# Low parts of feed-forward weights by an accumulating DMA instead of a VectorE subtraction

## The chip, the cores and the metric

The kernel runs on one core of a Trainium2 chip, in one launch. The metric is the device time of a run in microseconds; the median of three runs stands for a kernel.

## What is computed

Two layers of a diffusion block over 256 latent and 256 context tokens, 1024 wide, in float32. Each layer has a feed-forward, a mixer (attention, neighbourhood attention and a short convolution) and a second feed-forward; the context tokens take no part in the last feed-forward. Two conditioning vectors give scales, shifts and gates (`w_ada`). What the change touches is the feed-forward:

```python
def swiglu(u, wi, wo):
    g, up = jnp.split(u @ wi, 2, axis=-1)
    return (jax.nn.silu(g) * up) @ wo
...
h = post(h, swiglu(pre(h, m, 0, 0), ffn_wi[0], ffn_wo[0]), m, 0, 1, 0.5)
hc = post(hc, swiglu(pre(hc, mc, 0, 0), ffn_wi[0], ffn_wo[0]), mc, 0, 1, 0.5)
...
h = post(h, swiglu(pre(h, m, 6, 4), ffn_wi[1], ffn_wo[1]), m, 6, 5, 0.5)
if not last:
    hc = post(hc, swiglu(pre(hc, mc, 6, 4), ffn_wi[1], ffn_wo[1]), mc, 6, 5, 0.5)
```

The hidden width is 2816, that is 22 blocks of 128.

## The kernel before

Matrix products are made in the format float32r, which holds fewer bits than float32. So each float32 operand is split into a rounded half (high) and what rounding left over (low), and a product is three matmuls into one PSUM bank: high by high, low by high, high by low.

**Weights** come in units of 128 x 1024 elements (512 KB). A unit is a slot of a ring of eight (`next_slot`, tile `w`, 128 x 2 x 1024). `load_unit` brings the float32 unit into a staging buffer by a transfer on SyncE's queue (L91), ScalarE casts it to the rounded half `w[:, 0]` (L93), and VectorE subtracts that from the staging buffer into the low half `w[:, 1]` (L94). There are two staging buffers (`stg`), and in the last feed-forward three others (`stgx`). The transfer needs only a free staging buffer; the cast needs a free slot, which TensorE gives back after the last matmul that reads it.

**A feed-forward** (`ffn`) is called four times: over four token tiles (512 columns) for both of the first layer and the first of the second layer, and over two tiles (256 columns) for the last. The hidden blocks f go in groups of four. `up_all` loads the units of a pair of blocks (`load_up`: for each f the gate unit u = 0 and the value unit u = 1) and makes 24 matmuls for each unit. `down` multiplies a finished group of four blocks by its output weights, two units for each half of the output. Steadily the order is: up of two blocks (four units), down of a group (four units), up of two blocks (four units). The first four blocks are made otherwise: in the first two calls by `up_all`, in the last two by `up_first`, which takes eight token-major units (`wi_tm`) that fill the whole ring. Beside this VectorE accumulates the products of the conditioning (`ada_step`, L159 and L161) for the stages to come.

**Other engines.** GpSimd computes the reciprocal roots of the norms (L99, L111) and issues a few transfers (L192, L210). TensorE's transposes go through tiles `ptr`; PSUM banks are `mm` (3), `at` (2) and `pv` (1), taken in turn by the feed-forward. The order of instructions on every engine is chosen by a planner that simulates the kernel (`schedule_with_timeline_sim=True`); each engine then takes its instructions strictly in that order.

Of the kernel before, what the change touches and what calls it, by code (L numbers as in the profile page):

```python
# [8 lines left out]
F32 = mybir.dt.float32  # L9
F32R = mybir.dt.float32r  # L10
BF16 = mybir.dt.bfloat16
AF = mybir.ActivationFunctionType
ALU = mybir.AluOpType
# [12 lines left out]
def tile_hybrid_block(ctx: ExitStack, tc: tile.TileContext, xin, c2, w_ada, w_ada0, bcol, grow, gcol, win, qkg, bias_in,  # L26
                      convw, woa, wi, wi_tm, wo, ident, rope, out):
    nc = tc.nc
    pe, act, dve, pool, sp = nc.tensor, nc.scalar, nc.vector, nc.gpsimd, nc.sync
# [51 lines left out]
    def next_slot():  # L81
        return ring.tile([128, 2, 1024], F32R, name="w", tag="w")
# [3 lines left out]
    def load_unit(src):  # L86
        if more_stg:
            s = more_stg[0].tile([128, 1024], F32, name="stgx", tag="stgx", bufs=3)
        else:
            s = stg.tile([128, 1024], F32, name="stg", tag="stg")  # L90
        sp.dma_start(out=s, in_=src)  # L91
        w = next_slot()
        act.copy(w[:, 0], s)  # L93
        dve.tensor_tensor(out=w[:, 1], in0=s, in1=w[:, 0].bitcast(F32), op=ALU.subtract)  # L94
        return w

    def rsum(ss):
# [197 lines left out]
    def ffn(ph, l, i, U, tiles, after, ada_target, mode):  # L295
# [3 lines left out]
        ada0 = ada_done[0]  # L299

        def load_up(fs):
            return {(f, u): load_unit(wi[l, i, f, u]) for f in fs for u in range(2)}

        def up(fs, ws, segs, c0, n):
            pss = {(f, u): cur["mm"]() for f in fs for u in range(2)}
# [25 lines left out]
        def up_all(fs, mode=""):  # L331
            if mode == "k":
                segs = [(2 * qd, 2, lo_c, n_c) for qd in range(4)]
            elif mode[0:3] == "tok":
                segs = [(0, 8, 256, 256), (0, 8, 0, 256)]
            else:
                segs = [(0, 8, lo_c, n_c)]
            up(fs, load_up(fs), segs, lo_c, n_c)

        def load_down(f0, nf, hf):  # L340
            return [load_unit(wo[l, i, (f0 + fp) // 2, hf]) for fp in range(0, nf, 2)]
# [32 lines left out]
        def up_first():  # L374
            wt = [[load_unit(wi_tm[l, i, u, kp]) for kp in range(4)] for u in range(2)]
            for f in range(4):
                acts[f] = ph.tile([128, 2, n_c], F32R, name="a", tag="a", bufs=6)
            for t in tiles:
                c = slice(128 * t, 128 * t + 128)
                p = [tm_block(U, t, wt[u]) for u in range(2)]  # L380
                sg = ph.tile([128, 512], F32, name="sg", tag="sg")
                act.activation(sg, p[0], AF.Silu)
                dve.tensor_tensor(out=sg, in0=p[1], in1=sg, op=ALU.mult)
                pt = ps_tr.tile([128, 4, 128], F32, name="ptr", tag="ptr")
                for f in range(4):
                    pe.transpose(pt[:, f], sg[:, 128 * f:128 * f + 128], I)  # L386
                for f in range(4):
                    act.copy(acts[f][:, 0, c], pt[:, f])
                    dve.tensor_tensor(out=acts[f][:, 1, c], in0=pt[:, f], in1=acts[f][:, 0, c].bitcast(F32),
                                      op=ALU.subtract)  # L390
# [9 lines left out]
        for g, (f0, nf) in enumerate(FGROUPS[:-1]):  # L400
            f1 = f0 + nf
            if f1 < 20:
                up_all([f1, f1 + 1])
            elif len(tiles) == 4:
                wup = load_up([20, 21])
                up([20, 21], wup, [(0, 8, 256, 256)], 256, 256)
            else:
                up_all([20, 21])
            down(f0, nf, {}, [[(t, hf)] for hf in range(2) for t in tiles], g == 0, False)
            if f1 < 20:  # L410
                up_all([f1 + 2, f1 + 3])
# [379 lines left out]
```

## Time and profile before

| | |
|---|---|
| median of three runs | 1717.47 us (1716.42 to 1718.55) |
| profiled execution | 1717.2 us, span of the core 1715.4 us |
| mean granted TensorE clock | 0.995 |
| TensorE matmul, busy | 1684.8 us, 98% |
| VectorE, busy | 1200.1 us, 70% |
| ScalarE, busy | 715.0 us, 42% |
| GpSimd, busy | 49.0 us, 3% |
| DMA engines, SyncE's queue | 43.7% of 16 engines' span |

The time of the profiled execution is the span from the first to the last instruction and 1.8 us around it. Matmuls are pipelined and their ends are modelled, so TensorE's busy time shows where it had work, not how well it used it. A name such as L94 is a line of the kernel; `w<-stg,w` reads "tile w is written from tiles stg and w".

### The profile page before, as it was taken

How to read it: one execution, taken by the hardware profiler on the slowest of the kernel's cores; microseconds unless marked ns; L12 is line 12 of the kernel's file. 1: busy time of each engine (PE TensorE's matmuls, PEld its weight loads, DVE VectorE, ACT ScalarE, POOL GpSimd, SP SyncE). 2: the span in 40 equal slices, each digit the busy share in tenths (PEclk: the TensorE clock that was granted, in tenths of full speed). 3: DMA queues.
4: the chain of work that ended last, by engine and by line, in shares of the span. 5: the costliest groups of instructions: out<-in, count | busy, mean ns of one | idle time of the engine just before them, and what ended most of it. 6: DMA issues, size and time to landing. Idle time of an engine off the chain costs nothing.

```text
span 1715.4 us, 23300 instructions
## 1 busy us (share of the span) xinstructions
PE 1684.8 (98%) x9098; PEld 1413.9 (82%) x9098; DVE 1200.1 (70%) x1723; ACT 715.0 (42%) x1243; POOL 49.0 (3%) x76
## 2 busy tenths in 40 slices
PE   6999999999999999999999999999999999989997
PEld 4888888888877788888888888888888888769997
DVE  3578788877766675486686657889785768756664
ACT  5432222227656573322222354322222657765442
POOL 1000000002000010000000010000000110000000
PEclk9999999999999999999999999999999999999999
DMA  8566555523121334464443225656463323346551
GB/s 315 175 221 199 182 189 187 170 90 111 62 76 48 93 112 148 146 197 144 163 161 134 75 99 197 203 189 198 161 206 112 113 78 121 114 158 217 178 195 64
DMA packets 75613, 257.31 MB, mean 150 GB/s; under 512 B 10976, under 2 KB 14256, under 8 KB 74992
## 3 DMA queue, kind: packets, MB, share of 16 engines
q1 hardware_dynamic: 74304, 250.29, 43.7%
q0 software_dynamic: 1200, 5.55, 0.9%
q8 instruction: 71, 1.16, 0.3%
q14 instruction: 38, 0.31, 0.1%
HBM read 254.71 MB, written 1.09 MB: 149 GB/s over the span
## 4 chain that ended last, share of the span: by engine, by line
PE 96%; DMA 1%; DVE 1%; ACT 1%; issue 0%; POOL 0%; SPq 0%; DVEq 0%; POOLq 0%; ACTq 0%
PE mm L79 51%; PE at L79 27%; PE pv L79 15%; PE ptr L590 2%; PE ptr L234 1%; DMA GT<-in_qkg_dram 1%; DMA H<-in_xin_dram 0%; DMA stg<-in_wi_tm_dram 0%; DVE H L280 0%; DVE w L94 0%; ACT junk L217 0%; PE ptr L79 0%; PE ptr L471 0%; PE ptr L386 0%; ACT xn L229 0%
## 5 line engine op out<-in xcount | busy, mean ns | idle before, releaser
L79 PE MATMUL mm<-Uh,w 128*128 128x512 f32 (+1 forms) x1808 | 486.9, 348 | 0.0
L93 ACT CAST w<-stg 128x1024 fp32r<-128x1024 f32 x262 | 274.5, 1050 | 463.1 <-PE mm L79 398.4
L94 DVE TENSOR_TENSOR w<-stg,w 128x1024 fp32r<-128x1024 f32 x262 | 319.4, 1220 | 164.7 <-ACT w L93 163.9
L79 PEld LDWEIGHTS mm<-Uh,w 128*128 128x128 f32 x1808 | 318.7, 189 | 43.6 <-issue 1.9
L79 PE MATMUL mm<-Ul,w 128*128 128x512 f32 (+1 forms) x904 | 315.0, 348 | 0.0
L161 DVE SCALAR_TENSOR_TENSOR acc<-adas,S,acc 128x1024 f32<-128x1024 f32 x217 | 269.1, 1278 | 6.6 <-DMA adas<-in_w_ada_dram 6.3
L79 PE MATMUL at<-Uh,w 128*128 128x512 f32 (+1 forms) x960 | 253.7, 344 | 0.7 <-ACT Uh L272 0.7
L79 PE MATMUL mm<-w,a 128*128 128x512 f32 x924 | 228.1, 390 | 0.0
L79 PEld LDWEIGHTS mm<-w,a 128*128 128x128 f32 x924 | 173.1, 188 | 35.7
L79 PEld LDWEIGHTS mm<-Ul,w 128*128 128x128 f32 x904 | 171.2, 189 | 21.5 <-issue 0.5
L79 PEld LDWEIGHTS at<-Uh,w 128*128 128x128 f32 x960 | 168.9, 190 | 22.6 <-ACT Uh L272 0.9
L79 PE MATMUL mm<-w,Uh 128*128 128x512 f32 (+1 forms) x544 | 172.1, 389 | 0.0
L79 PE MATMUL at<-Ul,w 128*128 128x512 f32 (+1 forms) x480 | 165.4, 345 | 1.0 <-DVE Ul L273 1.0
L79 PE MATMUL at<-w,a 128*128 128x512 f32 x594 | 147.6, 391 | 0.0
L79 PEld LDWEIGHTS at<-w,a 128*128 128x128 f32 x594 | 110.8, 188 | 23.2 <-ACT a L325 0.8
L79 PE MATMUL pv<-Uh,w 128*128 128x512 f32 (+1 forms) x464 | 127.7, 353 | 0.0
L79 PEld LDWEIGHTS mm<-w,Uh 128*128 128x128 f32 x544 | 100.7, 188 | 19.8 <-issue 0.7
L94 DVE TENSOR_TENSOR w<-stgx,w 128x1024 fp32r<-128x1024 f32 x58 | 71.0, 1224 | 53.7 <-ACT w L93 53.6
L79 PE MATMUL mm<-w,Ul 128*128 128x512 f32 (+1 forms) x272 | 105.3, 387 | 0.9 <-DVE Ul L253 0.9
L320 DVE TENSOR_TENSOR sg<-mm,sg 128x512 f32<-128x512 f32 (+1 forms) x86 | 51.1, 594 | 75.4 <-PE mm L79 74.0
L79 PEld LDWEIGHTS at<-Ul,w 128*128 128x128 f32 x480 | 90.9, 189 | 12.6 <-DVE Ul L273 1.7
L79 PEld LDWEIGHTS pv<-Uh,w 128*128 128x128 f32 x464 | 82.7, 189 | 11.9
(162 smaller groups left out, 1807.9 us busy)
## 6 DMA issues: line engine op xcount, KB each, us to landing
adas<-in_w_ada_dram SPq DMA_DIRECT2D x144, 512.0 KB, 4.0
stg<-in_wi_dram SPq DMA_DIRECT2D x124, 512.0 KB, 4.2
stg<-in_wo_dram SPq DMA_DIRECT2D x66, 512.0 KB, 3.3
stg<-in_win_dram SPq DMA_DIRECT2D x40, 512.0 KB, 3.2
stgx<-in_wi_dram SPq DMA_DIRECT2D x36, 512.0 KB, 4.2
stgx<-in_wo_dram SPq DMA_DIRECT2D x22, 512.0 KB, 4.2
stg<-in_woa_dram SPq DMA_DIRECT2D x16, 512.0 KB, 3.3
stg<-in_wi_tm_dram SPq DMA_DIRECT2D x16, 512.0 KB, 3.3
```

The lines of the kernel that those rows point to most:

```text
L79: pe.matmul(out, lhsT=lhsT, rhs=rhs, start=first, stop=last)
L93: act.copy(w[:, 0], s)
L94: dve.tensor_tensor(out=w[:, 1], in0=s, in1=w[:, 0].bitcast(F32), op=ALU.subtract)
L161: dve.scalar_tensor_tensor(out=acc[:, v], in0=s, scalar=S[:, kt, v:v + 1], in1=acc[:, v], op0=ALU.mult, op1=ALU.add)
L234: pe.transpose(pt[:, b], xn[:, 128 * k:128 * k + 128], I)
L320: dve.tensor_tensor(out=sg[:, 0:n], in0=pss[f, 1][:, 0:n], in1=sg[:, 0:n], op=ALU.mult)
L590: pe.transpose(pt[:, b], P[:, 128 * b:128 * b + 128], I)
```

## The change

The value units (u = 1) of blocks 4 to 21 are loaded by a new function: 18 blocks in each of four calls, 72 of the 320 units. GpSimd's queue brings the unit straight into the slot's rounded half, being rounded in the transfer. ScalarE writes the negative of that half into the low half. A second transfer of the same unit from memory, also on GpSimd's queue, adds the float32 weights to it, so that what remains is the low part. No staging buffer and no VectorE instruction take part.

```diff
         dve.tensor_tensor(out=w[:, 1], in0=s, in1=w[:, 0].bitcast(F32), op=ALU.subtract)
         return w
 
+    def load_unit_dma(src):
+        w = next_slot()
+        pool.dma_start(out=w[:, 0], in_=src)
+        act.activation(w[:, 1], w[:, 0].bitcast(F32), AF.Copy, scale=-1.0)
+        pool.dma_start(out=w[:, 1], in_=src, accum_op=ALU.add)
+        return w
+
...
         def load_up(fs):
-            return {(f, u): load_unit(wi[l, i, f, u]) for f in fs for u in range(2)}
+            return {(f, u): (load_unit_dma if u and f >= 4 else load_unit)(wi[l, i, f, u])
+                    for f in fs for u in range(2)}
```

## Rows read from the trace of the kernel before

**Rows 1.** The page: busy time of each engine; the chain by engine.

```profile
PE 1684.8 (98%) x9098; PEld 1413.9 (82%) x9098; DVE 1200.1 (70%) x1723; ACT 715.0 (42%) x1243; POOL 49.0 (3%) x76
...
PE 96%; DMA 1%; DVE 1%; ACT 1%; issue 0%; POOL 0%; SPq 0%; DVEq 0%; POOLq 0%; ACTq 0%
```

**Rows 2.** Stretches: from:to, length, busy us of engines, clock, DMA share, GB/s.

```profile
28.00:1500.00 1472.00, 1469.64 (x7621) 1221.21 (x7622) 1070.28 (x1539) 596.93 (x1056) 39.23 (x57) 1.00 0.43 144
1500.00:1517.60 17.60, 12.16 (x62) 8.64 (x60) 13.14 (x22) 13.45 (x26) 3.36 (x4) 0.91 0.45 148
1517.60:1706.00 188.40, 188.38 (x1237) 173.56 (x1238) 105.61 (x135) 84.33 (x124) 0.55 (x1) 0.99 0.50 165
```

**Rows 3.** TensorE's waits, first and last of nine: total us, times, longest.

```profile
PE ptr L234 <- ACT xn L229: 12.5, 4, 10.0
...
PE at L79 <- DVE nmx L578: 0.4, 1, 0.4
```

**Rows 4.** Groups by line and shape: busy us, mean ns, idle before, releasers.

```profile
L94 DVE TENSOR_TENSOR w<-stg,w 128x1024 fp32r<-128x1024 f32 x262 | 319.4, 1220 | 164.7 <-ACT w L93 163.9
...
L93 ACT CAST w<-stg 128x1024 fp32r<-128x1024 f32 x262 | 274.5, 1050 | 463.1 <-PE mm L79 398.4 <-DMA stg<-in_wi_dram 25.0 <-DMA stg<-in_wo_dram 12.6
...
L229 ACT ACTIVATE xn<-H,rr 128x1024 f32<-128x1024 f32 x22 | 25.3, 1151 | 2.7 <-POOL rr L99 2.4
```

**Rows 5.** Groups by line on GpSimd.

```profile
L99 POOL TENSOR_TENSOR rr<-sst,NHALF 128x1 f32<-128x1 f32 x42 | 26.3, 627 | 695.0 <-DVE sst L104 694.9
...
L210 POOL DMA_DIRECT2D G<-dr x6 | 3.5, 579 | 16.0 <-DVE sst L104 11.3 <-DMA dr<-gr 4.7
```

**Rows 6.** DMA issues: queue, count, KB each, median us from issue to landing.

```profile
stg<-in_wi_dram SPq DMA_DIRECT2D x124, 512.0 KB, 4.2
...
G<-dr POOLq DMA_DIRECT2D x4, 1024.0 KB, 6.0
...
G<-dr POOLq DMA_DIRECT2D x2, 512.0 KB, 8.4
```

**Rows 7.** The chain that ended last, in order of time: start, us, what.

```profile
1082.95 5.44 PE at L79 x24
...
1505.66 4.53 DMA stg<-in_wi_tm_dram
...
1602.17 2.88 PE mm L79 x24
...
1619.45 2.88 PE mm L79 x24
...
1622.33 2.75 PE at L79 x12
```

**Rows 8.** ScalarE's casts of units in order of time: start, us; wait before.

```profile
1030.34 1.05 ACT L93 CAST w<-stg 128x1024 fp32r<-128x1024 f32 x1 [0.17 <-PE at L79]
...
1533.92 1.06 ACT L93 CAST w<-stgx 128x1024 fp32r<-128x1024 f32 x1 [0.30 <-PE at L79]
...
1538.34 1.05 ACT L93 CAST w<-stgx 128x1024 fp32r<-128x1024 f32 x1 [0.17 <-DMA stgx<-in_wi_dram]
...
1582.67 1.05 ACT L93 CAST w<-stgx 128x1024 fp32r<-128x1024 f32 x1 [1.55 <-PE mm L79]
...
1588.43 1.05 ACT L93 CAST w<-stgx 128x1024 fp32r<-128x1024 f32 x1 [1.55 <-PE mm L79]
...
1599.34 1.05 ACT L93 CAST w<-stgx 128x1024 fp32r<-128x1024 f32 x1 [0.31 <-PE mm L79]
```

**Rows 9.** TensorE in order of time: first matmuls of three units.

```profile
1044.57 0.48 PE L79 MATMUL mm<-Uh,w 128*128 128x512 f32 x1
...
1545.02 0.28 PE L79 MATMUL mm<-Uh,w 128*128 128x256 f32 x1
...
1551.41 0.28 PE L79 MATMUL mm<-Uh,w 128*128 128x256 f32 x1
```

**Rows 10.** Stretch of the last feed-forward, columns as in rows 2.

```profile
1545.00:1700.00 155.00, 155.00 (x1082) 145.55 (x1081) 88.94 (x110) 68.06 (x97) 0.00 (x0) 1.00 0.52 173
```

## The prediction

> **What bounds the kernel now.** I read the page first. TensorE is busy for 1684.8 us of a span of 1715.4, and the chain that ended last is 96% TensorE [rows 1]. The second view is the table of stretches, to find where the other 30.6 us are [rows 2]. From 28 us to 1500 us TensorE is busy for 1469.6 of 1472.0 us, and from 1517.6 to 1706 for 188.4 of 188.4. What is idle lies before 28 us, in 5.4 us at the entry of the last feed-forward, and behind 1706 us. The third view, TensorE's waits, has nine rows: ScalarE's normalised rows lead with 12.5 us, the last is 0.4 us, and none names a weight tile [rows 3]. So no matmul waits for a low part today, although VectorE is busy for 1200.1 us. The reader should take from this that VectorE's share, 70%, is no price: work taken off it is worth only what TensorE waits for, and TensorE waits for none of it.
>
> The idle stretch at 1500 us is in the chain as a weight load that landed late, 4.5 us for a token-major unit [rows 7]. Those units are not among the 72.
>
> **What the change removes.** 72 subtractions at 1220 ns [rows 4] are 72 x 1.22 = 87.8 us of VectorE, which falls from 1200 to about 1112 us. All are covered by TensorE, so the gain is 0. The 72 loads also leave the SyncE queue and the staging buffers, so the other units are fetched a little earlier; they wait for ring slots anyway (ScalarE's cast waited 398 us for matmuls to free slots [rows 4]). That is worth 0 too. Could the gain be more? The most that all idle time could give back is 30.6 us, and it lies where no such unit is loaded.
>
> **What it keeps and adds.** ScalarE exchanges a cast of 1050 ns for a scaled copy of the same 128 x 1024 elements; the nearest row is the scaled copy at 1151 ns [rows 4]. 72 x 0.1 = 7 us more on an engine that is 42% busy: 0. GpSimd gets 144 transfers to issue, at 579 ns for the transfers that it issues now [rows 5]: 144 x 0.58 = 84 us on an engine that is 3% busy. What is queued behind them there is the reciprocal root (L99) of each token tile, which the normalisation waits for. In the last feed-forward GpSimd does nothing at all between 1545 and 1700 us [rows 10], and in the others too the roots come at the ends, when the last of these units has long been loaded: 0, and if one root did fall behind a waiting transfer, the price would be that wait, a few us once.
>
> **What it makes longer.** Before, a slot that came free was full again after a cast and a subtraction, 1.05 + 1.22 = 2.3 us, because the transfer had gone ahead into a staging buffer. Now the slot itself is the target, so everything starts when TensorE lets go of it. Step by step:
> - issue of the first transfer: 0.58 us [rows 5]
> - its landing: the same unit from SyncE's queue takes 4.2 us, a 512 KB transfer from GpSimd's queue 8.4 us [rows 6]. I take 4.2: same source, same target, same shape. The 8.4 us one repeats a small block over all partitions.
> - ScalarE: 0 to 1.05 us behind a cast that has started, I take 0.5; then 1.05 to 1.15, I take 1.1
> - issue of the second transfer: 0.58 us
> - its landing: no row has an accumulating transfer. It cannot be shorter than the plain one, 4.2 us; above I take 8.4 us, the slowest 512 KB row. It reads 512 KB from memory and 512 KB of what is there, so it is nearest to the 1024 KB transfer from GpSimd's queue, 6.0 us [rows 6]. I take 6.0.
>
> Sum: 0.58 + 4.2 + 0.5 + 1.1 + 0.58 + 6.0 = 13.0 us. Low: 0.58 + 4.2 + 0 + 1.05 + 0.58 + 4.2 = 10.6. High: 0.58 + 8.4 + 1.05 + 1.15 + 0.58 + 8.4 = 20.2.
>
> **What time there is.** A unit's slot is that of the unit eight places before it. The moment it came free is the start of its cast where that waited for a matmul; the moment of need is the first matmul of the unit.
> - Feed-forwards over four tiles, steady: a unit takes TensorE 5.44 us [rows 7], and seven lie between: 38 us. Covered at 20.2 too.
> - Last feed-forward, steady (units of 2.9 us): of the four such units in a lap, the first has its slot at 1582.67 [rows 8] and is needed at 1602.17 [rows 7], 19.5 us; the last has it at 1599.34 and is needed at 1619.45, 20.1 us. Covered at 13.0; at 20.2 it is 0.7 us short.
> - Third feed-forward, first such unit (its slot held a token-major unit): free at 1030.34 [rows 8], needed at 1044.57 [rows 9]: 14.2 us. Covered at 13.0; short by 6.0 at 20.2.
> - Last feed-forward, first such unit: free at 1533.92 [rows 8], needed at 1545.02 [rows 9]: 11.1 us. Short by 13.0 - 11.1 = 1.9 us; by 9.1 at 20.2; not short at 10.6. The second has 1538.34 to 1551.41, 13.1 us, plus the delay of the first: covered.
>
> So the forecast is one stall of 1.9 us: 1717.2 us (the profiled execution, 1.8 us more than its span, and 0.3 under the median of the three) + 1.9 = 1719.1 us. It is written as 1719.0, and the low end of the sum is 1717.2. What is late next after such a stall: nothing, since TensorE's delay moves every later need with it.
>
> The Trainium skill (DMA: Bandwidth & Descriptors, section on the anatomy of one DMA on the gpsimd path) fits such a transfer as about 2.0 us plus its bytes at 436 GB/s, which is 3.2 us for 512 KB. By that the chain would be 0.58 + 3.2 + 0.5 + 1.1 + 0.58 + 3.2 = 9.2 us as an estimate from that page, under 11.1, and the time 1717.2 us. The trace does not agree for the one queue: its 512 KB row says 8.4 us [rows 6].
>
> **Rivals.**
> 1. *The chain is long, and TensorE stalls at the two entries and a little in each lap* (slower). At 20.2 us: 6.0 + 9.1 at the entries, and 0.7 us in each of 155 / 22.6 = 6.9 turns of the ring, 4.8 us (a lap of eight up and four down units lasts from 1588.43 [rows 8] to 1622.33 [rows 7], 33.9 us; the ring's eight units are 22.6 of that). Sum 19.9: 1737.1 us. It is over 0.2% once the chain passes about 14.4 us (3.3 us short at the last entry, 0.2 at the third). For it: 8.4 us stands in the trace, and the second transfer has no row. Against it: a plain unit lands in 4.2.
> 2. *The transfers fill the last feed-forward* (slower). There the 16 DMA engines are 52% busy at 173 GB/s [rows 10], so a plain unit of 0.524 MB costs 0.524 / (173 / 0.52) = 1.57 us of all of them. 0.48 x 155 = 74 us are left, and about 16 accumulating transfers must fit: 4.6 us each, 2.9 times a plain one. At two times (one stream more to read) the share is 0.52 + 16 x 3.1 / 155 = 0.84 and nothing happens; at four times it is 16 x 6.3 + 81 = 182 us for 155, +27 us: 1744 us. A form of it is GpSimd's order: if each second transfer is issued before the next unit's first, four units occupy its queue for four times the way from issue to issue, 4 x 7.0 = 28 us of a lap of 34. It fits while that way is under 8.5 us; with the first landing in 8.4 it is 4 x 11.8 = 47 us, and 155 / 34 laps x 13 = +59 us.
>    The Trainium skill (DMA: Bandwidth & Descriptors, section on issuing engines not being separate DMA queues) says that transfers from all queues end up on the same 16 engines and interleave, so a move to GpSimd's queue buys no bandwidth. Nothing in the trace of before tests it.
> 3. *A gain* (faster). With VectorE lighter and the order of all engines planned anew, the 5.4 us of idle TensorE at the entry of the last feed-forward could close: 1717.2 - 5.4 = 1711.8 us. For it: two subtractions sit in that part of the chain. Against it: what is longest there is a landing, and it is not of these units.
> 4. *The planner reorders TensorE* so that a later unit's matmuls go first where one is late. Then the forecast's 1.9 us vanish: 1717.2 us. It ends inside the forecast.
>
> **Chances.** Forecast with rival 4 (0 to 3.4 us more): 0.52. Rival 1: 0.23. Rival 2: 0.15. Rival 3: 0.10, and some of that is under 0.2%. 0.2%, 3.4 us, is about what a measurement here can tell from no change. Faster 0.09, same 0.53, slower 0.38. The range goes from 1714.0 (beyond it lies most of rival 3) to 1738.0 (all of rival 1, a part of rival 2), which leaves some 0.08 below and 0.10 above. The likeliest case alone has 1716.5 to 1720.6.
>
> **What would show it.** VectorE near 1112 us, TensorE's busy time unchanged, GpSimd with 144 transfers more, memory reads up by 72 x 0.524 = 38 MB. First transfers landing in 4 to 5 us and second in 6; matmuls of the first such unit in the last feed-forward starting about 2 us after the unit before has ended, and nowhere else waiting for a transfer. The forecast is wrong if TensorE waits for accumulating transfers in every lap of the last feed-forward (rivals 1 and 2: the share of the DMA engines tells which), if a second transfer takes over 8 us, or if the idle time at 1500 us changes.

## The result, and the profile after

The changed kernel takes 1739.03 us (median of four runs, 1737.64 to 1740.27) against 1717.6 us beside it: ratio 1.0126, interval 1.0111 to 1.0141. That is slower by 21.4 us and 1 us above the prediction's range. The profiled execution took 1737.9 us, with a span of 1736.2, 20.8 more than before.

The page of the changed kernel, answering [rows 1]: busy time by engine, GpSimd's DMA queue (packets, MB, share of 16 engines), and the chain by engine.

```profile
PE 1691.1 (97%) x9098; PEld 1418.1 (82%) x9098; DVE 1116.4 (64%) x1651; ACT 710.9 (41%) x1243; POOL 149.7 (9%) x220
...
q0 software_dynamic: 21936, 81.06, 19.7%
...
PE 78%; DMA 8%; issue 7%; DVE 4%; ACT 1%; POOL 1%; SPq 0%; POOLq 0%; DVEq 0%; ACTq 0%
```

VectorE fell to 1116 us, as the sum said. TensorE has the same 9098 matmuls, but the chain is only 78% TensorE now. TensorE's waits, answering [rows 3], name what is new:

```profile
PE mm L79 <- DMA w<-in_wi_dram: 9.2, 6, 3.6
PE ptr L79 <- DVE rd L182: 5.4, 2, 3.9
```

The first is what was feared: six times, all in the last feed-forward, a matmul waits for an accumulating transfer. The second was not foreseen: a small matmul of the conditioning (`ada_finish`) waits twice for VectorE's sums. Behind the waits the clock falls. The table of stretches of the changed kernel, columns as in [rows 2]:

```profile
1091.00:1094.50 3.50, 3.50 (x10) 2.76 (x9) 0.56 (x2) 1.06 (x1) 0.85 (x1) 0.54 0.49 172
...
1560.00:1654.00 94.00, 89.87 (x617) 83.58 (x615) 35.52 (x47) 38.78 (x54) 15.61 (x22) 1.00 0.79 225
1654.00:1661.00 7.00, 5.64 (x27) 5.64 (x28) 0.43 (x2) 0.00 (x0) 0.00 (x0) 0.51 1.02 304
...
1695.00:1699.00 4.00, 4.00 (x23) 4.00 (x22) 0.00 (x0) 0.00 (x0) 0.00 (x0) 0.58 1.05 337
```

The granted clock is about half, 1.2 instead of 2.4 GHz, in three stretches at the longest waits (of 3.9, 3.6 and 2.5 us), where TensorE is busy but slow. The stretch from 1654 us begins with the end of its wait, so only its busy 5.64 us count here. That costs about 3.5 x 0.46 + 5.64 x 0.49 + 4.0 x 0.42 = 6.1 us; TensorE's busy time grew by 1691.1 - 1684.8 = 6.3 us. 9.2 + 5.4 + 6.1 = 20.7 us, for the 20.8 us by which the span grew.

**How a weight comes late.** Transfers to their landing in the last feed-forward, from 1560 to 1720 us: first the first transfers (L99), with who waited for them; then the accumulating ones (L101).

```profile
  ACT w L100: 64.0, 12
...
DMA to landing us min/median/max: 6.9/8.8/10.5
```

```profile
  PE mm L79: 8.4, 5
...
DMA to landing us min/median/max: 5.6/6.3/8.0
```

The accumulating transfer lands in 6.3 us, where 6.0 was taken. The first one takes 8.8 us, where 4.2 was taken. GpSimd and ScalarE around the longest weight wait, in order of time (start, us, and the wait before):

```profile
1623.28 0.85 POOL L101 DMA_DIRECT2D w<-in_wi_dram  x1 [10.41 <-ACT w L100]
1624.87 0.55 POOL L99 DMA_DIRECT2D w<-in_wi_dram  x1 [0.74 <-PE mm L79]
1638.56 0.85 POOL L101 DMA_DIRECT2D w<-in_wi_dram  x1 [13.14 <-ACT w L100]
1639.14 1.40 POOL L99 DMA_DIRECT2D w<-in_wi_dram  x2
1649.55 0.89 POOL L101 DMA_DIRECT2D w<-in_wi_dram  x1 [9.01 <-ACT w L100]
```

```profile
1632.36 1.05 ACT L93 CAST w<-stgx 128x1024 fp32r<-128x1024 f32 x1 [4.93 <-DMA stgx<-in_wi_dram]
...
1635.03 0.41 ACT L333 CAST a<-sg 128x256 fp32r<-128x256 f32 x1 [1.34 <-DVE sg L328]
...
1636.27 1.04 ACT L93 CAST w<-stgx 128x1024 fp32r<-128x1024 f32 x1
1637.21 1.06 ACT L100 ACTIVATE w<-w 128x1024 fp32r<-128x1024 f32 x1
...
1648.19 1.06 ACT L100 ACTIVATE w<-w 128x1024 fp32r<-128x1024 f32 x1 [7.90 <-DMA w<-in_wi_dram]
```

And TensorE: first the last matmul of the unit eight places before, which frees the slot; then the unit whose first transfer was the one of 1639.14:

```profile
1631.73 0.28 PE L79 MATMUL mm<-Uh,w 128*128 128x256 f32 x1
...
1651.53 0.28 PE L79 MATMUL mm<-Ul,w 128*128 128x256 f32 x1
1655.36 0.80 PE L79 MATMUL mm<-Uh,w 128*128 128x256 f32 x2 [3.56 <-DMA w<-in_wi_dram]
```

Follow it backwards. The matmul of 1655.36 needs the transfer issued at 1649.55, which needs the negative copy of 1648.19, which needs the first transfer of 1639.14. GpSimd issued that one, and another with it, right behind the 1638.56 one. It had stood for 13.1 us before a transfer that waited for ScalarE's copy of 1637.21. The transfer which that copy reads, the one of 1624.87, had landed much earlier, at 1632.1:

```profile
DMA to landing us min/median/max: 7.2/7.2/7.2
```

But ScalarE takes its instructions in order, and before the copy stood two casts of staged units and three small instructions, two of which waited for VectorE, 1.3 and 0.6 us. So the copy came 5.1 us late, and a unit's first transfer is held back by another unit's second.

In numbers for this unit: its slot is free at 1632.0. From there it is 7.1 us to the issue of its first transfer, 9.0 to the start of its copy, 1.4 to the issue of its second transfer and 5.8 to the matmul: 23.3 us. TensorE wanted it 19.8 us after 1632.0. Without the 7.1 us it would have been in time, and so it would with a first landing of 4.2 us.

**How the sums come late.** VectorE and then TensorE in the third feed-forward:

```profile
1083.35 2.48 DVE L168 SCALAR_TENSOR_TENSOR acc<-adas,S,acc 128x1024 f32<-128x1024 f32 x2 [2.73 <-DMA adas<-in_w_ada_dram]
...
1089.14 1.21 DVE L182 TENSOR_REDUCE rd<-uf 128x32 f32<-128x1024 f32 x1
```

```profile
1090.40 0.26 PE L79 MATMUL ptr<-rd,SEL 128*32 128x16 f32 x8 [3.90 <-DVE rd L182]
```

The conditioning loads (`adas`) between 1055 and 1090 us land as follows, in the kernel before and then in the changed one:

```profile
DMA to landing us min/median/max: 3.3/4.2/4.5
```

```profile
DMA to landing us min/median/max: 3.2/5.4/7.5
```

VectorE has time, but not the data; TensorE, which takes its instructions in order, stands before a matmul of 16 columns. The planner has a part in it too. In the kernel before, VectorE's last sum and TensorE's matmul were 3.0 us apart:

```profile
1084.34 1.20 DVE L175 TENSOR_REDUCE rd<-uf 128x32 f32<-128x1024 f32 x1
...
1088.54 0.26 PE L79 MATMUL ptr<-rd,SEL 128*32 128x16 f32 x8
```

With a lighter VectorE the plan sets this matmul 17 places earlier in TensorE's order (the 5573rd of 9098 instead of the 5590th), so that this slack is gone.

### The profile page after: what moved, and what is told of

Its sections match the earlier page's. It is cut to its first block, busy times and chain, and to the rows that moved or that the text cites. A ratio compares the mean times of both kernels' runs of the same rounds, so it can differ in the third digit from the quotient of the medians.

```text
span 1736.2 us, 23387 instructions
## 1 busy us (share of the span) xinstructions
PE 1691.1 (97%) x9098; PEld 1418.1 (82%) x9098; DVE 1116.4 (64%) x1651; ACT 710.9 (41%) x1243; POOL 149.7 (9%) x220
## 4 chain that ended last, share of the span: by engine, by line
PE 78%; DMA 8%; issue 7%; DVE 4%; ACT 1%; POOL 1%; SPq 0%; POOLq 0%; DVEq 0%; ACTq 0%
PE mm L79 43%; PE at L79 21%; PE pv L79 12%; DMA w<-in_wi_dram 4%; DMA adas<-in_w_ada_dram 2%; PE ptr L598 2%; DVE acc L168 1%; DMA GT<-in_qkg_dram 1%; PE ptr L241 1%; DVE w L94 1%; DMA stg<-in_wo_dram 1%; POOL w L101 0%; ACT w L100 0%; ACT w L93 0%; DMA H<-in_xin_dram 0%
## 5 line engine op out<-in xcount | busy, mean ns | idle before, releaser
L94 DVE TENSOR_TENSOR w<-stg,w 128x1024 fp32r<-128x1024 f32 x208 | 253.7, 1221 | 209.0 <-ACT w L93 207.9
L93 ACT CAST w<-stg 128x1024 fp32r<-128x1024 f32 x208 | 217.5, 1049 | 220.6 <-PE mm L79 164.5
L100 ACT ACTIVATE w<-w 128x1024 fp32r<-128x1024 f32 x72 | 76.4, 1062 | 302.1 <-DMA w<-in_wi_dram 292.6
L79 PEld LDWEIGHTS mm<-Ul,w 128*128 128x128 f32 x904 | 172.8, 191 | 21.4 <-issue 0.5
L333 ACT CAST a<-sg 128x512 fp32r<-128x512 f32 (+1 forms) x86 | 46.8, 544 | 172.1 <-DVE sg L328 171.3
L94 DVE TENSOR_TENSOR w<-stgx,w 128x1024 fp32r<-128x1024 f32 x40 | 48.9, 1224 | 93.6 <-ACT w L93 93.6
L79 PEld LDWEIGHTS at<-Ul,w 128*128 128x128 f32 x480 | 91.4, 190 | 13.5 <-DVE Ul L280 2.4
```

Of the source, the lines that this page charges most:

```text
L79: pe.matmul(out, lhsT=lhsT, rhs=rhs, start=first, stop=last)
L100: act.activation(w[:, 1], w[:, 0].bitcast(F32), AF.Copy, scale=-1.0)
L333: act.copy(a[:, 0, c], sg[:, 0:n])
```

## The experiments

**1. The new loading only over four tiles.**

```diff
-            return {(f, u): (load_unit_dma if u and f >= 4 else load_unit)(wi[l, i, f, u])
+            return {(f, u): (load_unit_dma if u and f >= 4 and len(tiles) == 4 else load_unit)(wi[l, i, f, u])
```

> The new loading only in the three feed-forwards over four tiles (54 units), the old one in the last. Theory (two separate causes: 7 us from TensorE waiting for VectorE's conditioning sums in the first and third feed-forward, 14 us from late units in the last): the first 7 us stay and the last feed-forward is as before, 1724 to 1725 us. Rival (all of it comes from the last feed-forward, the early 7 us are given back at its entry): 1717 to 1719 us.

Measured: 1723.42 us (ten runs, 1717.4 to 1729.2), ratio 1.0032, 1.0018 to 1.0045; +5.9 us. No weight wait; the sums were waited for:

```profile
PE ptr L79 <- DVE rd L182: 3.5, 2, 3.2
```

The first cause stands by itself, a little smaller than expected. It scatters more than the kernel before does. The profiled execution was a short one, 1717.8 us, so its 3.5 us are not what the median shows; that the 5.9 us are the waits for the sums is inferred from the run having no other new wait.

**2. The new loading only in the last feed-forward** (`len(tiles) == 2` in place of 4).

> The new loading only in the last feed-forward (18 units). Theory: no wait for the conditioning sums, 1717.5 + 14 = 1731 to 1733 us, with TensorE waiting 8 to 10 us for accumulating transfers. Rival (the early delay shifts the entry and makes the late units worse): under 1727 us.

Measured: 1732.53 us, ratio 1.0087, 1.0071 to 1.0103; +15.0 us. The weight wait is there, the wait for sums is not.

```profile
PE mm L79 <- DMA w<-in_wi_dram: 6.7, 6, 3.2
```

(The trace is of the shortest of the four runs, 1728.7 us.)

5.9 + 15.0 = 20.9 of the 21.4 us: two causes that add up. The rival of a shifted entry falls.

**3. Low half by a negative copy alone.**

```diff
...
+        sp.dma_start(out=s, in_=src)
         w = next_slot()
-        pool.dma_start(out=w[:, 0], in_=src)
+        act.copy(w[:, 0], s)
         act.activation(w[:, 1], w[:, 0].bitcast(F32), AF.Copy, scale=-1.0)
-        pool.dma_start(out=w[:, 1], in_=src, accum_op=ALU.add)
```

The lines left out here (`...`), as in experiments 5 and 7, take the staging buffer `s`.

> The 72 units are staged and cast as before, and their low half is only the negative copy on ScalarE: no second transfer, no GpSimd, no subtraction (the low parts are left out, so the output is another). VectorE is as light as in the changed kernel, the DMA traffic as before. Theory (the conditioning sums are late because the planner, seeing a light VectorE, put TensorE's matmul for them earlier): TensorE waits some us for the sums, 1720 to 1724 us. Rival (they are late because the transfers slow the conditioning loads): no wait, 1717 to 1718 us.

Measured: 1717.97 us, ratio 1.0005, 0.9996 to 1.0015. TensorE waits 0.4 us for the sums:

```profile
PE ptr L79 <- DVE rd L186: 0.4, 1, 0.4
```

So the theory that the plan alone makes the sums late falls: it uses up the slack (the matmul is the 5577th here), and no more. The run also measures the gain directly: 72 subtractions less are worth nothing, 0.7 us at most by the interval.

**4. Traffic that nobody waits for.**

```diff
+    JUNK = 2
...
+        w = load_unit(src)
+        for _ in range(JUNK):
+            x = dpool.tile([128, 1024], F32, name="jx", tag="jx")
+            pool.dma_start(out=x, in_=src)
+        return w
```

> The old loading everywhere, and beside each of the 72 units two transfers of the same 512 KB on GpSimd's queue into a scratch in memory that nobody reads. The traffic is at least that of the changed kernel, but no weight waits for it. Theory (the last feed-forward is late by the order of waits on GpSimd and long landings, not by full DMA engines): the last feed-forward is as before within 2 us; the conditioning loads may be slower, 1717 to 1724 us in all. Rival (the DMA engines are the limit there): TensorE waits for staged units and conditioning in every lap, 1730 to 1745 us.

Measured: 1910.77 us, ratio 1.1125. It does not tell the two theories apart. Nothing tied these transfers to the ring, so GpSimd issued them all early; from memory to memory each took long to land, and the conditioning loads of the first stage starved:

```profile
jx<-in_wi_dram POOLq DMA_DIRECT2D x144, 512.0 KB, 14.5
```

```profile
PE at L80 <- DMA adas<-in_w_ada_dram: 73.6, 8, 28.1
PE mm L80 <- DMA adas<-in_w_ada_dram: 48.3, 8, 8.0
```

What it shows is that traffic on GpSimd's queue delays loads on SyncE's.

**5. The first transfer back ahead of the slot.** The accumulation stays.

```diff
...
+        sp.dma_start(out=s, in_=src)
         w = next_slot()
-        pool.dma_start(out=w[:, 0], in_=src)
+        act.copy(w[:, 0], s)
         act.activation(w[:, 1], w[:, 0].bitcast(F32), AF.Copy, scale=-1.0)
         pool.dma_start(out=w[:, 1], in_=src, accum_op=ALU.add)
```

> The first transfer goes back to SyncE's queue and a staging buffer, with the cast on ScalarE; then the negative copy and the accumulating transfer as in the changed kernel, for all 72 units. The bytes moved and the accumulation are those of the changed kernel; the way from free slot to full slot loses the first landing (1.05 + 1.06 + 0.86 + about 6 = 9 us against lookaheads of 11 and 19). Theory (the last feed-forward is late because first transfers start only at the free slot and land late behind second ones): no wait for weights there, and only the delays of the conditioning sums remain, 1719 to 1726 us. Rival (the DMA engines are full there, or the accumulation is too slow in itself): 1732 to 1740 us.

Measured: 1728.04 us, ratio 1.0065, 1.0050 to 1.0080; a little above the theory's range, below the rival's. No weight wait in any feed-forward; 4.4 us for the sums. The profiled execution's span is 9.0 us longer than before: 4.4 of them are this wait, 2.3 are more busy time of TensorE, whose granted clock was 0.59 from 1090.4 to 1094.4 us, behind the wait, and 2.3 are spread over other idle time. So the median's 10.5 us, more than experiment 1's 5.9, are explained only in part. In the stretch of the last feed-forward the DMA engines are fuller than in the changed kernel, 0.87, and TensorE is busy throughout:

```profile
1560.00:1700.00 140.00, 140.00 (x990) 132.11 (x989) 63.44 (x86) 80.34 (x109) 13.61 (x16) 1.00 0.87 245
```

So full DMA engines are not what stops TensorE there. What the accumulation costs can be worked out: 13.3% of this execution's span in GpSimd's queue,

```profile
q0 software_dynamic: 11568, 43.30, 13.3%
```

is 0.133 x 1724.4 = 229 us of all 16 engines; less the 0.9% of 1715.4 = 15 us that the queue takes in the kernel before, for 72 transfers: 2.97 us each, 1.9 times the 1.57 us of a plain unit.

**6. Both first transfers of a pair ahead of its second ones on GpSimd.**

```diff
+            w0 = next_slot()
+            pool.dma_start(out=w0[:, 0], in_=wi[l, i, fs[0], 1])
...
+            w1 = next_slot()
+            ins = pool.dma_start(out=w1[:, 0], in_=wi[l, i, fs[1], 1])
...
+            with tc.issue_after(ins.ins):
+                for w, f in ((w0, fs[0]), (w1, fs[1])):
+                    pool.dma_start(out=w[:, 1], in_=wi[l, i, f, 1], accum_op=ALU.add)
```

> As the changed kernel, but on GpSimd both first transfers of a pair of blocks are issued before the second transfer of either. Theory (the order on GpSimd, where a second transfer that waits for ScalarE holds back the next unit's first, is the larger part of the last feed-forward's 14 us): 1726 to 1732 us. Rival (the landings themselves are too long, whatever the order): 1737 to 1741 us.

Measured: 1727.20 us, ratio 1.0055, 1.0035 to 1.0075. Weights are waited for once, and the sums as before or longer:

```profile
PE ptr L79 <- DVE rd L175: 7.8, 2, 5.1
...
PE mm L79 <- DMA w<-in_wi_dram: 0.9, 1, 0.9
```

GpSimd in a lap of the last feed-forward (L306 and L310 are first transfers, L314 second ones):

```profile
1629.60 0.55 POOL L306 DMA_DIRECT2D w<-in_wi_dram  x1 [8.97 <-PE mm L79]
1635.36 0.54 POOL L310 DMA_DIRECT2D w<-in_wi_dram  x1 [5.21 <-PE mm L79]
1636.74 0.87 POOL L314 DMA_DIRECT2D w<-in_wi_dram  x1 [0.84 <-DVE w L94]
1640.82 0.54 POOL L306 DMA_DIRECT2D w<-in_wi_dram  x1 [3.21 <-PE mm L79]
```

Every first transfer of this lap now waits for TensorE to free its slot and for nothing else, and so do 16 of the 18 of this feed-forward; the row of 13.1 us has no counterpart, the longest wait for ScalarE is 5.0 us. The first transfers of the second unit of a pair now land thus in the last feed-forward:

```profile
DMA to landing us min/median/max: 4.4/5.7/6.3
```

They are shorter once they are not issued in a bunch behind an accumulating one. The accumulating transfers (L314), which are now issued behind first ones, take longer instead, 8.4 us where they took 6.3:

```profile
DMA to landing us min/median/max: 5.5/8.4/9.6
```

So a first and a second landing together are hardly shorter (14.1 against 15.1 us). What the new order takes away is the time for which a first transfer stood behind another unit's second.

**7. The first transfer alone,** with the staged unit and VectorE's subtraction.

```diff
...
+        sp.dma_start(out=s, in_=src)
         w = next_slot()
         pool.dma_start(out=w[:, 0], in_=src)
-        act.activation(w[:, 1], w[:, 0].bitcast(F32), AF.Copy, scale=-1.0)
-        pool.dma_start(out=w[:, 1], in_=src, accum_op=ALU.add)
+        dve.tensor_tensor(out=w[:, 1], in0=s, in1=w[:, 0].bitcast(F32), op=ALU.subtract)
```

> The first transfer is that of the changed kernel (rounding, GpSimd's queue, into the free slot); the unit is staged besides by SyncE's queue, and VectorE subtracts as before. No accumulation and no wait for ScalarE on GpSimd. Theory (a first transfer is long only where it is queued behind an accumulating one): first transfers land in 4 to 5 us in the last feed-forward too, no wait for weights, 1717 to 1721 us. Rival (a rounding transfer from GpSimd's queue takes 8 us or more there by itself): landings of 8 us and more, and some waits at the entry, 1720 to 1726 us.

Measured: 1721.23 us, ratio 1.0022, 1.0012 to 1.0032. No weight wait, one wait of 2.0 us for the sums. The transfers land in 5.5 us at the median of the whole run, between theory and rival (5.1 in the last feed-forward):

```profile
w<-in_wi_dram POOLq DMA_DIRECT2D x72, 512.0 KB, 5.5
...
q0 software_dynamic: 11568, 43.30, 8.1%
```

(8.1% of 1720.2 - 15.4) / 72 = 1.72 us of the engines, near a plain unit: rounding in the transfer is almost free, adding is not.

**8. An eighth of the accumulation.**

```diff
-        pool.dma_start(out=w[:, 1], in_=src, accum_op=ALU.add)
+        pool.dma_start(out=w[:, 1, 0:128], in_=src[:, 0:128], accum_op=ALU.add)
```

> As the changed kernel, with the accumulating transfer cut to 128 of 1024 columns (the other low parts stay the negative of the rounded half, so the output is another). All waits are kept, the accumulated bytes are an eighth. Theory (what lengthens first landings and conditioning loads is the engine time of the accumulations): first transfers land in 4 to 5 us, the last feed-forward loses under 4 us, the waits for conditioning sums go, 1717 to 1722 us. Rival (the dependent steps themselves, issue, wait, landing, are too many, whatever the bytes): 1730 us or more.

Measured: 1716.28 us, ratio 0.9993, 0.9984 to 1.0002. Every step of the changed kernel that has to wait for another is still there, and none costs anything: neither weights nor sums appear among TensorE's waits. First transfers land in

```profile
DMA to landing us min/median/max: 3.9/4.5/6.6
```

in the last feed-forward, and conditioning loads between 1055 and 1090 us in

```profile
DMA to landing us min/median/max: 3.7/4.2/4.7
```

near the 3.3/4.2/4.5 of the kernel before. So the number of steps is not the trouble by itself: without most of the accumulated bytes they fit. A second transfer of full size that only copies was not run, so the adding and the bytes that it reads are not told apart.

**9. Experiment 6 in the last feed-forward alone** (`load_up` takes the old way where `len(tiles) == 4`).

> The new loading only in the last feed-forward (18 units), with both first transfers of a pair issued before its second ones; the old loading elsewhere. Theory (in the last feed-forward the order on GpSimd decides): of the 15 us that the same 18 units cost in the old order at most 3 are left, 1717 to 1721 us. Rival (the order helped only together with the traffic of the earlier feed-forwards): 1726 to 1733 us.

Measured: 1718.94 us, ratio 1.0012, 1.0004 to 1.0021: +1.5 us where experiment 2 cost 15.0 with the same 18 units. One weight wait of 0.8 us is left. The order on GpSimd is 13.5 of the 15 us. Experiment 8 removed the weight waits in the old order, and this one nearly removes them with all the bytes: the loss needs both, as the sum of 23.3 us said for one unit.

**10. Experiment 6 in the second feed-forward of each layer.**

> The new loading in the second feed-forward of each layer (36 units), first transfers ahead, the old loading in the first ones. Theory (the sums of the conditioning are late only in the first and third feed-forward, where TensorE comes to their matmul early): 1717 to 1721 us, not clear of the kernel before, though 36 subtractions and their staging are gone. Rival (the delay of the sums only moves to another feed-forward): 1722 us or more.

Measured: 1718.84 us, ratio 1.0008, 1.0000 to 1.0016. No wait for the sums; one for a weight, in a profiled execution that was the slowest of the twelve (1723.7 us):

```profile
PE mm L79 <- DMA w<-in_wi_dram: 2.9, 1, 2.9
```

36 subtractions fewer, and still nothing gained: no version here that makes all the low parts is faster than the kernel before.

## Why the prediction was wrong

- *The gain is 0*: right, and shown by experiment 3 (1.0005).
- *The chain from free slot to full slot*: its ends held, its middle did not. Taken and measured in the last feed-forward: second landing 6.0 and 6.3 us; scaled copy 1.1 and 1.06; issue of the first 0.58 and 0.55, of the second 0.58 and 0.86. The step that failed is the landing of the first transfer: "I take 4.2: same source, same target, same shape". It measured 8.8 us, above even the 8.4 that was its upper bound. Here the landing went by what was queued with the transfer, not by its shape: 4.5 us without the accumulated bytes (experiment 8), 5.7 in another order (experiment 6).
- *ScalarE, 0.5 us*: too small. The copy of 1637.21 came 5.1 us after its transfer had landed, behind five other instructions. That is most of the 7.1 us by which the next unit's first transfer was late.
- *No step for the order on GpSimd*: the forecast let every first transfer start when its slot was free; the one followed above started 7.1 us after that. The time that it set against the chain was right: 19.5 to 20.1 us there, 19.8 measured. The danger stood in rival 2 with its limit, 8.5 us from issue to issue and 11.8 us with a landing of 8.4; the measured distances were 13.7 us (1624.87 to 1638.56) and 10.4 (1639.14 to 1649.55). The mechanism was priced and then put among the 0.15, because the landing had been taken short. Experiments 6 and 9 show that it is the larger part.
- *Where the stall would be*: the entries of the third and last feed-forward were thought tightest. At the third entry no weight was waited for, and at the last the wait was 0.7 us; the laps behind it, thought covered, had the rest. Rival 1's 1737.1 us is near the result by luck: its 15.1 us at the two entries were 0.7.
- *Full DMA engines (rival 2, first form)*: the estimate of two times a plain unit was good (1.9) and its share too (0.84 said, 0.79 from 1560 to 1654 us), and "at two times nothing happens" holds for that bound: at 0.87 TensorE did not stop (experiment 5). But the step looked only at whether the bytes fit. Longer landings were its price, for the first transfers and for loads that the change does not touch.
- *The conditioning*: no step spoke of the loads on SyncE's queue that share the engines. It is +5.9 us (experiment 1). Traffic is necessary for it: experiments 3 and 8 have the same lighter VectorE without it, and a wait of 0.4 us or none. The new plan adds to it by taking away the 3.0 us of slack. Traffic without the lighter VectorE does less: in experiment 7, with VectorE as busy as before (1197 us), TensorE waits 2.0 us for the sums. How the 5.9 us divide was not measured.
- *The clock*: what a wait costs after it has ended, 6.1 us here, was in no term.

## What to carry to other kernels

Work taken off an engine for which nobody waits is worth nothing, and what it is exchanged for can still cost: here DMA time, which every load in flight pays in longer landings. Before moving a dependent pair of transfers to an in-order queue, write down the order in which that queue will hold them; a second transfer that waits for another engine holds back the next unit's first, and putting the firsts ahead was worth 13.5 us. A landing time read from a quiet stretch need not hold in a busier one: the same first transfers took 4.5 us at the median in experiment 8 and 8.8 in the changed kernel.

## What was not expected of the hardware

- An accumulating transfer of 512 KB into SBUF took 2.97 us of the 16 DMA engines, a rounding one 1.72, a plain one 1.57. GpSimd needed 0.86 us to issue it, and 0.55 us for the rounding one (medians in the changed kernel).
- Three waits of TensorE of 2.5 to 3.9 us were followed by 3.5 to 5.6 us of work at about half the granted clock, so that they cost 10.0 us and then 6.1 more. Not every such wait was: in experiment 1 a wait of 3.2 us ended at 1087.1 us, and the granted clock from 1087 to 1095 us was 1.00.
- With the same order of issue and the same steps, an eighth of the accumulated bytes brought the median landing of the first transfers from 8.8 to 4.5 us in the last feed-forward, though the 16 DMA engines of the changed kernel were 0.79 busy on average from 1560 to 1654 us, not full.
